# A hybrid decoder layer on one core: first key tiles finished in turn, short products between input steps, log-decay rows spread by DMA

## The chip, the cores and the metric

The kernel runs on one core of a Trainium2 chip. The metric is the time on the device in microseconds, the median of several runs; lower is better. The engines are TensorE (PE in the profile, PEld for its weight loads), VectorE (DVE), ScalarE (ACT), GpSimd (POOL) and SyncE (SP), whose queue issues all DMAs. Each engine takes its own instructions in the order in which they stand in the program, and waits at an instruction until the semaphores it names have been raised.

## What is computed

One layer of a decoder trunk for 1024 tokens of width 1024, all in float32. The part that matters here is the input projection and the preparation of the gated delta rule (4 heads of width 128):

```python
h = rmsnorm(x, norm1_w)
proj = h @ w_in                       # q, k, v, z (512 each), b, a (4 each), then 3 x 512 for mixer B
qkv_a = silu(causal_dwconv(qkv_a, conv_qkv_w))            # four taps
qa, ka = l2norm(q) * 128 ** -0.5, l2norm(k)
beta = sigmoid(b_a)
g = -exp(a_log) * softplus(a_a + dt_bias)                 # log decay per token and head
o_a = gated_delta_rule(qa, ka, va, g, beta)
...
gc = cumsum(g) within a chunk
dec = exp(gc[t] - gc[j]) for t >= j, else 0
lmat = strict(dec) * (k k^T) * beta                       # then a triangular solve, a scan over chunks
```

Behind it come dilated attention over the same projection, the output projection with a residual, a second norm, a gated MLP with a short convolution, a residual and a final norm.

## The kernel before

**Products.** Activations lie transposed, features on the partitions. A float32 product is made of three passes: operands are split into a rounded high part and a rest (`split`, lines 189 to 191; `split_x`), and `mm3` (lines 183 to 187) multiplies high x high, high x low and low x high into one bank of PSUM. In the profile such a pass is a `128x512` MATMUL of about 0.4 us that starts every 0.23 us, here called a wide product. Products that are not split (`mm`, `tp`) run as two passes for a float32 product and one for a transpose.

**The order of the work.** The program is recorded by generators which a small planner, `Weave` (lines 41 to 113), steps in turn. Each generator yields how long it wants to wait; the planner keeps an estimate of TensorE's time (`pe`) and of when each tile is ready, and runs the ready generator of the lowest level. `until(name)` waits for a named event, `need(tile)` gives the estimated wait for a tile, `slack` adds to it. What is recorded on TensorE stands in that order in the program (`TOKEN` is stamped on every product). The other engines' orders are made by a scheduler, so they aren't always those of the source.

**The first stage.** `first` (lines 313 to 321) multiplies the first three key column tiles: for each of the 8 feature tiles `k` it goes through the 3 tiles and 2 halves of the tokens (`pst`, six banks), so all six banks end with the last `k`. That is 144 wide products. Between them come, at levels 0 and 1:

- `norms` (lines 327 to 344): sums the squares over the features with products by a column of ones (`ssp`, 8 products of one column), takes the reciprocal root on POOL (`rst`), transposes it to rows over all partitions (8 transposes) and copies it to `rstdB`.
- `gates` (lines 351 to 388): the projection of the 8 gate columns (`wba`), evicted to `barow`, turned by 8 products with `sel`, then `beta` and `g` on DVE and ACT, and a product with the triangle `tri` that gives the running sums `gc`, with tokens on the partitions.

**Keys.** When `first` and `norms` are done, `dense` (line 438) adds `first_keys` (lines 431 to 436): the three pairs of banks are scaled by `rstdB` into `xr`, then each is put through `conv_silu` (lines 402 to 415): one ACT copy with a scale (the first tap), three DVE taps, a tanh on ACT, and a DVE step that makes `kT`. `dense` itself goes on with the other columns of the projection (`DENSE`, lines 37 and 38: key 3, two columns of mixer B, then q and v of head 0 and so on), 48 wide products each, in the two banks `hf`; the first of them are also the first two banks of `pst`.

`kprep` (lines 496 to 551), one for each head, waits for `gates` and makes the decay matrix `dec`: the head's `gc` is spread over all partitions by 8 TensorE transposes into two `atr` banks; ACT adds the negated `gc` as a bias, chunk by chunk; `gel`, the last column, is copied by DVE; POOL masks; ACT takes the exponential. Then `tokens` (lines 477 to 494) transposes `kT` through two more `atr` banks; ACT evicts each bank to `ktok` and takes four squares with sums from it (`sq`, into `ssk`). Then `kT` is multiplied with itself (two banks, four products each) and DVE makes `um` with `bp` and `dec`; four DMAs write its blocks to `mdram`. When all four heads are done, `forward_sub` solves the blocks on DVE. The tag `atr` has two banks in all: a new bank waits for the last reader of the bank before the last.

Of the kernel before, what the change touches and what calls it, by code (L numbers as in the profile page):

```python
# [7 lines left out]
F32 = mybir.dt.float32  # L8
F32R = mybir.dt.float32r
AF = mybir.ActivationFunctionType  # L10
# [5 lines left out]
P = 128  # L16
S = 1024
KT = 8
H = 4
NCH = 8  # L20
FT = 22
NEG = -1.0e30
EPS = 1e-6
SLOTS = {"kT": 2, "kU": 2, "dv": 2, "dw": 2, "kt": 4, "uy": 5, "qa": 4, "ev": 2, "go": 2, "Xa": 7, "Xb": 9}
TURNS = {"kT*": ("kT", "kU"), "dv*": ("dv", "dw"), "X": ("Xa",) * 7 + ("Xb",) * 9}
# [109 lines left out]
def hybrid_layer(tc, I, out):  # L135
# [14 lines left out]
    def tile_(pool, shape, dt, name, tag, bufs):  # L150
        return wv.slot(pool.tile(list(shape), dt, name=name, tag=tag, bufs=bufs), tag, bufs)
# [23 lines left out]
    def mm(dst, lhs, rhs, us, start=True, stop=True, **kw):  # L175
        tc.stamp_issue_order_token(nc.tensor.matmul(dst, lhs, rhs, start=start, stop=stop, **kw).ins, TOKEN)  # L176
        wv.product(us, dst, lhs, rhs)

    def tp(dst, src):
        tc.stamp_issue_order_token(nc.tensor.transpose(dst, src, ident).ins, TOKEN)  # L180
        wv.product(0.11, dst, src)

    def mm3(dst, lhs, rhs, first, last, **kw):
        us = 0.2135 * rhs[0].shape[-1] / 512
        mm(dst, lhs[0], rhs[0], us, first, False, **kw)
        mm(dst, lhs[0], rhs[1], us, False, False, **kw)
        mm(dst, lhs[1], rhs[0], us, False, last, **kw)
# [25 lines left out]

    mixer = dp.tile([8, P, S], F32, name="mixer")
    mdram = dp.tile([H, 32, 1024], F32, name="mdram")
    xdram = dp.tile([H, 32, 1024], F32, name="xdram")
    xtdram = dp.tile([H, 32, 1024], F32, name="xtdram")
    apark = dp.tile([4, 3, P, S], F32, name="apark")
# [8 lines left out]
    def next_bank(tag, *tiles, slack=0.0):  # L227

        while max(wv.need(*tiles), wv.slot_free(tag, 2)) + slack > 1e-3:
            yield max(wv.need(*tiles), wv.slot_free(tag, 2)) + slack  # L230
        return bank(tag)

    def half(i):
        return slice(i * 512, i * 512 + 512)

    def v8(t):
        return t.rearrange("p (c t) -> p c t", c=NCH)
# [73 lines left out]
    pst = [bank(t) for t in ("hf", "asc", "ch") for _ in range(2)]  # L311

    def first():
        for k in range(KT):
            w = wk0[k // 2]
            for i in range(6) if k else (0, 2, 4, 1, 3, 5):
                yield wv.need(*xs[k], *w)
                m, h = divmod(i, 2)
                wm = [t[:, k % 2, m * P:(m + 1) * P] for t in w]
                mm3(pst[i], wm, [t[:, half(h)] for t in xs[k]], k == 0, k == KT - 1)  # L320
        wv.done.add("first")


# [3 lines left out]
    def norms():  # L327
        yield wv.need(acc, slack=10.0)
        ssp = yield from next_bank("atr", acc)
        for c in range(NCH):  # L330
            mm(ssp[:, c:c + 1], acc[:, c * P:(c + 1) * P], ones[:, :1], 0.215)
            if c % 2:
                yield 0.4
        ve.tensor_scalar(rst, ssp[:, :NCH], 1.0 / 1024, EPS, op0=OP.mult, op1=OP.add)
        rsqrt(rst, rst, NCH)
        wv.done.add("rst")
        yield wv.need(rst)
        for h in range(2):
            pb = yield from next_bank("atr")
            for c in range(4):  # L340
                i = 4 * h + c
                tp(pb[:, c * P:(c + 1) * P], rst[:, i:i + 1].to_broadcast([P, P]))
            ve.tensor_copy(rstdB[:, half(h)], pb)
        wv.done.add("norms")
# [6 lines left out]
    def gates():  # L351

        yield wv.need(wba, xts[-1], slack=4.0)
        for h in range(2):
            pt = yield from next_bank("atr", wba, xts[-1])
            for k in range(KT):
                o = 32 * (k % 4)
                mm(pt[o:o + 32], wba[:, k, :], xts[k][:, half(h)], 0.3, k < 4, k >= 4, tile_position=(0, o))
            ac.activation(barow[:, half(h)], pt, AF.Copy)
        pt = yield from next_bank("atr", barow)  # L360
        for c in range(NCH):
            mm(pt[:, c * 8:(c + 1) * 8], barow[:, c * P:(c + 1) * P], sel, 0.215)
        yield from wv.until("rst")
        ba = sp.tile([P, NCH, 8], F32, name="ba")
        ve.tensor_tensor(ba, pt[:, :64].rearrange("p (c j) -> p c j", c=NCH),
                                rst[:, :, None].to_broadcast([P, NCH, 8]), op=OP.mult)
        ac.activation(beta, ba[:, :, :H], AF.Exp, scale=-1.0)
        ve.tensor_scalar(beta, beta, 1.0, None, op0=OP.add)
        ve.reciprocal(beta, beta)
        zt = sp.tile([P, NCH, H], F32, name="zt")  # L370
        ve.tensor_tensor(zt, ba[:, :, H:], dtb[:, None, :].to_broadcast([P, NCH, H]), op=OP.add)
        az = sp.tile([P, NCH, H], F32, name="az")
        ac.activation(az, zt, AF.Abs)
        ac.activation(az, az, AF.Exp, scale=-1.0)
        ac.activation(az, az, AF.Ln, bias=1.0)
        ve.scalar_tensor_tensor(az, zt, 0.0, az, op0=OP.max, op1=OP.add)
        ea = sp.tile([P, H], F32, name="ea")
        ac.activation(ea, alog, AF.Exp)
        g = sp.tile([P, NCH, H], F32, name="g")
        ve.scalar_tensor_tensor(g, az, -1.0, ea[:, None, :].to_broadcast([P, NCH, H]), op0=OP.mult,  # L380
                                       op1=OP.mult)
        pt = yield from next_bank("atr", g)
        mm(pt[:, :NCH * H], tri, g.rearrange("p c h -> p (c h)"), 0.215)
        ve.tensor_copy(gc, pt[:, :NCH * H].rearrange("p (c h) -> p c h", c=NCH))
        ve.tensor_scalar(ngc, gc, -1.0, None, op0=OP.mult)
        ac.activation(ngam, gc, AF.Exp)
        ve.tensor_scalar(ngam, ngam, -1.0, None, op0=OP.mult)
        wv.done.add("gates")
# [39 lines left out]
    T = {}  # L428
    gated = {}

    def first_keys():
        xr = [scaled(pst[2 * h:2 * h + 2], "xr", tag=("ev", "ev", "qa")[h]) for h in range(3)]
        for h in range(3):
            T["k", h] = conv_silu(xr[h], 4 + h, "kT", "kT*")
            wv.add(3, kprep(h))
            yield wv.need(T["k", h])

    def dense():

        yield from wv.until("first")  # L440
        yield from wv.until("norms")
        wv.add(2, first_keys())
        nxt = None
        for i, col in enumerate(DENSE):
            kind, h = col[:2]
            if kind == "z":
                yield from wv.until(("o", h))
            w = nxt or wk(I["wi"][i])
            if i + 1 < len(DENSE):
                nxt = wk(I["wi"][i + 1])  # L450
            pair = []
            for hh in range(2):
                pt = bank("hf")
                yield wv.need(pt, *w)
                for k in range(KT):
                    mm3(pt, [t[:, k, :] for t in w], [t[:, half(hh)] for t in xs[k]], k == 0, k == KT - 1)
                    yield 0.0
                pair.append(pt)
            if kind == "k":
                T["k", h] = conv_silu(pair, 4 + h, "kT", "kT*")  # L460
                wv.add(3, kprep(h))
            elif kind == "q":
                q = conv_silu(pair, h, "qT", "qa")
                wv.add(4, qprep(h, q))
            elif kind == "v":
                v = conv_silu(pair, 8 + h, "vT", "qa")
                wv.add(4, vprep(h, v))
            elif kind == "z":
                og = gated[h] = A("og", "kT*")
                sy.dma_start(og, mixer[h])  # L470
                ve.tensor_tensor(og, og, silu2(pair, "zz"), op=OP.mult)
            else:
                sy.dma_start(apark[h, col[2]], scaled(pair, "aqkv", True))
                wv.done.add(col)
        wv.done.add("dense")
# [20 lines left out]
    def kprep(h):  # L496
# [5 lines left out]
        dec = A("dec", ("dv", "dw")[h % 2])  # L502
        gend = small("gend")
        gel = small("gel")
        for hh in range(2):
            c0 = 4 * hh
            pg = yield from next_bank("atr")
            for c in range(4):
                tp(pg[:, c * P:(c + 1) * P], gc[:, c0 + c, h:h + 1].to_broadcast([P, P]))
            pv = pg.rearrange("p (c t) -> p c t", c=4)  # L510
            for c in range(4):
                ac.activation(v8(dec)[:, c0 + c, :], pv[:, c, :], AF.Identity, bias=ngc[:, c0 + c, h:h + 1])
            ve.tensor_copy(gel[:, c0:c0 + 4], pv[:, :, P - 1])
        po_.affine_select(v8(dec), v8(dec), pattern=[[0, NCH], [1, P]], compare_op=OP.is_ge, fill=NEG,
                                base=0, channel_multiplier=-1)
        ve.tensor_tensor(gend, gel, gc[:, :, h], op=OP.subtract)
# [958 lines left out]
```

## Time and profile before

| | |
|---|---|
| median of three runs | 1268.12 us (1267.27 to 1270.15) |
| the profiled execution: time, span | 1267.09 us, 1263.9 us |
| its mean granted TensorE clock | 0.992 |

A run of a profile lists busy time by engine, the span in 40 slices, the chain of work that ended last, and groups of instructions. Line 131 is the helper that records every DVE, ACT, POOL and SP operation, line 176 the one for products and line 180 the one for transposes, so instructions are told apart by their tiles: `kT<-xr,gcw,kT` is a tap of the convolution, `sq<-ps` a square with its sum, `dec<-ps,ngc` the decay with its bias, `xr<-ps,rstdB` the scaling.

The stage that the change touches lies in the first 120 us. Busy time of each engine there, in us, and TensorE's granted clock, from the view of windows:

| window, us | PE | DVE | ACT | clock |
|---|---|---|---|---|
| 20 to 30 | 9.84 | 9.30 | 5.61 | 1.00 |
| 30 to 40 | 9.05 | 2.20 | 2.01 | 0.74 |
| 40 to 50 | 10.00 | 2.93 | 3.06 | 0.92 |
| 50 to 60 | 10.00 | 10.00 | 6.71 | 1.00 |
| 60 to 70 | 8.03 | 10.00 | 8.38 | 0.95 |
| 70 to 80 | 10.00 | 8.68 | 4.52 | 0.88 |
| 80 to 90 | 10.00 | 5.69 | 4.87 | 1.00 |

All the waits of TensorE in the whole span sum to some 16 us; the largest are 2.8 us for `w` of the chunk chains, 2.1 for the second norm, 2.0 in the last product and 2.0 for `xr`, which is at 66 us.

### The profile page before, as it was taken

To read this page: it belongs to the slowest core of one execution; us is meant where nothing else is said; L and a number is where in the kernel's file an instruction comes from. 1 tells how busy PE (TensorE), PEld (TensorE's weight loads), DVE (VectorE), ACT (ScalarE), POOL (GpSimd) and SP (SyncE) were. 2 spreads that over 40 slices of the span, in tenths; PEclk is the share of its full clock that TensorE was granted. 3 is DMA by queue.
4 is the path that set the end of the run, shared out by engine and by line. 5 is a ranking of instruction groups with operands and counts; after the bars stand their busy time and mean duration, and the time that the engine had idled before them with its cause. 6 is when DMAs were issued, how large, how long until landed. Compare 5 with 4: busy or idle time off the path is not lost.

```text
span 1263.9 us, 18352 instructions
## 1 busy us (share of the span) xinstructions
PE 1240.5 (98%) x7102; PEld 1010.7 (80%) x7102; DVE 940.6 (74%) x1450; ACT 587.5 (46%) x1122; POOL 45.3 (4%) x34
## 2 busy tenths in 40 slices
PE   9999999999999999999999999999999999999996
PEld 7878887888677767878888888888888888787886
DVE  7575984573554455576888988988988979899875
ACT  7355534363544253365554444445445444343541
POOL 0012010022000000000000000000000000000000
PEclk9899999999999999999999999999999999999998
DMA  7022243345322411444323123123122198455623
GB/s 232 28 59 76 101 121 98 134 151 201 103 81 93 141 53 41 126 150 150 117 67 100 60 90 100 56 95 101 53 98 100 50 339 311 149 158 191 199 85 134
DMA packets 77766, 151.41 MB, mean 120 GB/s; under 512 B 21744, under 2 KB 28528, under 8 KB 77680
## 3 DMA queue, kind: packets, MB, share of 16 engines
q1 hardware_dynamic: 77680, 150.25, 36.1%
q8 instruction: 55, 0.90, 0.3%
q14 instruction: 31, 0.25, 0.1%
HBM read 112.21 MB, written 35.91 MB: 117 GB/s over the span
## 4 chain that ended last, share of the span: by engine, by line
PE 81%; DVE 8%; DMA 5%; issue 3%; ACT 2%; SPq 0%; POOL 0%; POOLq 0%; DVEq 0%; ACTq 0%
PE ps L176 42%; PE pa L176 18%; PE pc L176 9%; PE dw L176 8%; PE ps L180 4%; DMA wd<-in_wd 2%; DVE pr L131 2%; DMA r<-upark 1%; DVE x1h L131 1%; DVE kT L131 1%; DVE wd L131 1%; DVE r L131 0%; DMA wst<-in_wu 0%; DVE xr L131 0%; DMA xt<-in_xT 0%
## 5 line engine op out<-in xcount | busy, mean ns | idle before, releaser
L176 PE MATMUL dw<-pr 128*128 128x512 f32 (+1 forms) x984 | 213.4, 377 | 2.8 <-DVE x1h L131 2.0
L176 PEld LDWEIGHTS dw<-pr 128*128 128x128 f32 x984 | 176.1, 188 | 39.1 <-DVE x1h L131 4.2
L176 PE MATMUL ps<-xhi,whi 128*128 128x512 f32 x448 | 187.5, 419 | 2.0 <-DVE xr L131 2.0
L176 PE MATMUL ps<-xhi,wlo 128*128 128x512 f32 x448 | 177.0, 395 | 0.2 <-DVE wlo L131 0.2
L176 PE MATMUL ps<-xlo,whi 128*128 128x512 f32 x448 | 176.4, 394 | 0.0
L176 PE MATMUL pa<-T,pair 128*128 128x512 f32 x528 | 128.6, 393 | 0.7 <-ACT u L131 0.7
L176 PEld LDWEIGHTS pa<-T,pair 128*128 128x128 f32 x528 | 99.8, 189 | 21.8 <-ACT u L131 1.0
L176 PEld LDWEIGHTS ps<-xhi,whi 128*128 128x128 f32 x448 | 85.5, 191 | 19.4 <-issue 3.1
L176 PEld LDWEIGHTS ps<-xhi,wlo 128*128 128x128 f32 x448 | 85.0, 190 | 19.4 <-DVE wlo L131 0.6
L176 PEld LDWEIGHTS ps<-xlo,whi 128*128 128x128 f32 x448 | 85.7, 191 | 13.9
L131 ACT ACTIVATE u<-pa 128x512 f32<-128x512 f32 x44 | 26.3, 599 | 110.6 <-PE pa L176 110.6
L131 DVE SCALAR_TENSOR_TENSOR y<-xu,fcw,y 128x1023 f32<-128x1023 f32 (+1 forms) x44 | 56.4, 1281 | 25.7 <-ACT y L131 25.6
L131 ACT ACTIVATE whi<-wst 128x1024 fp32r<-128x1024 f32 (+2 forms) x38 | 38.6, 1016 | 68.8 <-PE ps L176 58.3
L176 PE MATMUL pa<-B,A 128*128 128x512 f32 x264 | 63.4, 389 | 0.0
L176 PE MATMUL pc<-T,S 128*128 128x512 f32 x264 | 63.4, 389 | 0.0
L176 PE MATMUL pa<-T,S 128*128 128x512 f32 x264 | 63.4, 389 | 0.0
L176 PE MATMUL pc<-B,pair 128*128 128x512 f32 x264 | 63.4, 389 | 0.0
L131 ACT ACTIVATE sm<-sm,mx 128x512 f32<-128x512 f32 (+2 forms) x64 | 41.5, 649 | 42.4 <-DVE mx L131 42.4
L131 DVE TENSOR_TENSOR wst<-wst 128x512 f32<-128x512 f32 x88 | 60.4, 686 | 0.8
L176 PE MATMUL ps<-B,pair 128*128 128x512 f32 x252 | 60.5, 389 | 0.0
L176 PEld LDWEIGHTS pc<-B,pair 128*128 128x128 f32 x264 | 49.6, 188 | 10.3
L176 PEld LDWEIGHTS pa<-B,A 128*128 128x128 f32 x264 | 49.6, 188 | 10.3
(233 smaller groups left out, 2280.4 us busy)
## 6 DMA issues: line engine op xcount, KB each, us to landing
wst<-in_wu SPq DMA_DIRECT2D x44, 512.0 KB, 3.6
wd<-in_wd SPq DMA_DIRECT2D x44, 512.0 KB, 4.0
wst<-in_wi SPq DMA_DIRECT2D x25, 512.0 KB, 3.7
upark<-y SPq DMA_DIRECT2D x22, 512.0 KB, 3.5
apark<-aqkv SPq DMA_DIRECT2D x12, 512.0 KB, 2.9
r<-upark SPq DMA_DIRECT2D x11, 512.0 KB, 7.9
r<-upark SPq DMA_DIRECT2D x22, 256.0 KB, 7.0
wa<-in_wd SPq DMA_DIRECT2D x22, 256.0 KB, 2.7
```

The costliest lines, as they stand in the source:

```text
L131: return getattr(eng, op)(*a, **kw)
L176: tc.stamp_issue_order_token(nc.tensor.matmul(dst, lhs, rhs, start=start, stop=stop, **kw).ins, TOKEN)
L180: tc.stamp_issue_order_token(nc.tensor.transpose(dst, src, ident).ins, TOKEN)
```

## The change

1. `first` takes its 144 wide products in another order: for the first five feature tiles (`TOGETHER`) as before, then key tile by key tile through the last three. The banks of tile 0 end 36 products before those of tile 2. As soon as a tile's second bank has ended, `first_key` for this head is added to the planner; it waits for `norms`, scales, convolves, and adds `kprep`. `first_keys` and its place in `dense` are gone.
2. In `norms` the 8 products with `ones` yield 0.6 us after each one (before: 0.4 us after each second one); in `gates` the 8 products with `sel` do too (before: none between them), and wait 2 us more for `barow`.
3. `gates` makes `gc` a second time with tokens along the row, by a product with the operands exchanged (32 rows: chunk and head). ACT evicts it to `grow`, and a DMA writes it to `gdram` in memory (16 KB). `kprep` no longer transposes: one DMA for each head reads the head's 8 rows of 512 bytes for all 128 partitions (a step of 0 over the partitions) into `dec`, 512 KB. `gel` is copied from there, and ACT adds the bias in place.

Computed values stay the same.

```diff
+TOGETHER = 5
...
+    gdram = dp.tile([NCH * H, P], F32, name="gdram")
...
     def first():
-        for k in range(KT):
+        steps = [(k, i) for k in range(TOGETHER) for i in (range(6) if k else (0, 2, 4, 1, 3, 5))]
+        steps += [(k, 2 * m + h) for m in range(3) for k in range(TOGETHER, KT) for h in range(2)]
+        for k, i in steps:
             w = wk0[k // 2]
-            for i in range(6) if k else (0, 2, 4, 1, 3, 5):
-                yield wv.need(*xs[k], *w)
-                m, h = divmod(i, 2)
-                wm = [t[:, k % 2, m * P:(m + 1) * P] for t in w]
-                mm3(pst[i], wm, [t[:, half(h)] for t in xs[k]], k == 0, k == KT - 1)
+            yield wv.need(*xs[k], *w)
+            m, h = divmod(i, 2)
+            wm = [t[:, k % 2, m * P:(m + 1) * P] for t in w]
+            mm3(pst[i], wm, [t[:, half(h)] for t in xs[k]], k == 0, k == KT - 1)
+            if k == KT - 1 and h == 1:
+                wv.add(2, first_key(m))
         wv.done.add("first")
...
             mm(ssp[:, c:c + 1], acc[:, c * P:(c + 1) * P], ones[:, :1], 0.215)
-            if c % 2:
-                yield 0.4
+            yield 0.6
...
+        yield wv.need(barow, slack=2.0)
         pt = yield from next_bank("atr", barow)
         for c in range(NCH):
             mm(pt[:, c * 8:(c + 1) * 8], barow[:, c * P:(c + 1) * P], sel, 0.215)
+            yield 0.6
...
-        mm(pt[:, :NCH * H], tri, g.rearrange("p c h -> p (c h)"), 0.215)
+        g32 = g.rearrange("p c h -> p (c h)")
+        mm(pt[:, :NCH * H], tri, g32, 0.215)
+        mm(pt[:NCH * H, P:2 * P], g32, tri, 0.215)
+        grow = tile_(sp, [NCH * H, P], F32, "grow", "osq", 1)
+        ac.activation(grow, pt[:NCH * H, P:2 * P], AF.Copy)
+        sy.dma_start(gdram, grow)
...
-    def first_keys():
-        xr = [scaled(pst[2 * h:2 * h + 2], "xr", tag=("ev", "ev", "qa")[h]) for h in range(3)]
-        for h in range(3):
-            T["k", h] = conv_silu(xr[h], 4 + h, "kT", "kT*")
-            wv.add(3, kprep(h))
-            yield wv.need(T["k", h])
+    def first_key(h):
+        yield from wv.until("norms")
+        xr = scaled(pst[2 * h:2 * h + 2], "xr", tag=("ev", "ev", "qa")[h])
+        T["k", h] = conv_silu(xr, 4 + h, "kT", "kT*")
+        wv.add(3, kprep(h))
 
     def dense():
         yield from wv.until("first")
         yield from wv.until("norms")
-        wv.add(2, first_keys())
...
-        for hh in range(2):
-            c0 = 4 * hh
-            pg = yield from next_bank("atr")
-            for c in range(4):
-                tp(pg[:, c * P:(c + 1) * P], gc[:, c0 + c, h:h + 1].to_broadcast([P, P]))
-            pv = pg.rearrange("p (c t) -> p c t", c=4)
-            for c in range(4):
-                ac.activation(v8(dec)[:, c0 + c, :], pv[:, c, :], AF.Identity, bias=ngc[:, c0 + c, h:h + 1])
-            ve.tensor_copy(gel[:, c0:c0 + 4], pv[:, :, P - 1])
+        rows = gdram.rearrange("(c h) t -> h c t", h=H)[h]
+        sy.dma_start(v8(dec), bass.AP(tensor=rows.tensor, offset=rows.offset, ap=[[0, P]] + list(rows.ap)))
+        ve.tensor_copy(gel, v8(dec)[:, :, P - 1])
+        for c in range(NCH):
+            ac.activation(v8(dec)[:, c, :], v8(dec)[:, c, :], AF.Identity, bias=ngc[:, c, h:h + 1])
```

## The prediction

> **What bounds the kernel now.** I read the page first: its engine table, its slices, its chain of waits. Columns of the first rows: busy us, share of the span, instructions.
>
> ```profile
> span 1263.9 us, 18352 instructions
> PE 1240.5 (98%) x7102; PEld 1010.7 (80%) x7102; DVE 940.6 (74%) x1450; ACT 587.5 (46%) x1122; POOL 45.3 (4%) x34
> PEclk9899999999999999999999999999999999999998
> PE 81%; DVE 8%; DMA 5%; issue 3%; ACT 2%; SPq 0%; POOL 0%; POOLq 0%; DVEq 0%; ACTq 0%
> ```
>
> TensorE sets the time: a microsecond put into its stream or taken out of it shows at the end, and what other engines do costs nothing unless TensorE waits for it. The clock is below full in slices 1 and 2, where the change lies, so I took TensorE's timeline there (start, duration, engine, form; in brackets the idle time before and who ended it):
>
> ```profile
> 31.41 1.95 PE L176 MATMUL ps<-sel,barow 128*128 128x8 f32 x16 [0.95 <-ACT barow L131]
> 35.40 0.63 PE L176 MATMUL ps<-xlo,whi 128*128 128x512 f32 x1
> 35.82 0.63 PE L176 MATMUL ps<-xhi,wlo 128*128 128x512 f32 x1
> 42.63 1.03 PE L180 MATMUL ps<-ident,rst 128*128 128x128 f32 x8
> 52.65 1.03 PE L180 MATMUL ps<-ident,gc 128*128 128x128 f32 x8
> 53.44 0.47 PE L176 MATMUL ps<-xhi,whi 128*128 128x512 f32 x1
> 65.33 0.66 PE L180 MATMUL ps<-ident,kT 128*128 128x128 f32 x4
> 67.95 0.50 PE L176 MATMUL ps<-xhi,whi 128*128 128x512 f32 x1 [1.97 <-DVE xr L131]
> 115.74 0.47 PE L176 MATMUL ps<-xhi,whi 128*128 128x512 f32 x1
> ```
>
> I count the wide products (128x512) of the input projection from the start. An undisturbed one takes 0.227 us (start to start). After 0.95 us of idling and 16 short `sel` instructions they take 0.427, from 34.8 to 41.4; after 1.97 us of idling again, from 68.8 to 72.1. Product 144, the last of the first three key tiles, ends at 52.65. Product 337 starts at 115.74: by then all four heads' keys are turned and multiplied in either version. That is my common mark.
>
> **What the change removes on TensorE.** (a) Sixteen one-column and eight-column products now stand one or two between steps of three wide ones. I take 0.2 us each (group of two `ones` at 33.22 to 33.67: 0.225; at 34.44 to 34.82: 0.19) and 0.09 for each return to wide products (33.67 to 33.98 is 0.31 instead of 0.227). From 29.96: two steps of 0.97, six of 1.17, two of 0.97 and one of 0.68 bring TensorE to the `rst` transposes at 41.5 (before 42.6); 0.87 for those, nine products, 0.43 for the two `tri` products (the new one by the nearest row, a 128-wide `kT` product at 0.2) and 18 products end product 144 at 49.1 (before 52.65): 3.5 gained, if the clock holds. (b) The `gc` transposes go: 2 x 0.88 and 4 x 0.45 = 3.6. (c) The 1.97 wait and its slow stretch (eleven products and four transposes, some 1.9) go: 3.9. Together 11.0.
>
> **What it adds: the order.** In the changed program's order, whose waits can be read off it, head 0's eight `kT` transposes stand on TensorE directly behind product 144, and product 145, the first of the next column, behind them. Before, 48 wide products and eight `gc` transposes stood there, 12.7 us of cover. TensorE takes them in order, and the first waits for DVE's last step on `kT`. When is that? DVE's timeline of before gives the prices:
>
> ```profile
> 43.27 1.29 DVE L131 COPY rstdB<-ps 128x512 f32<-128x512 f32 x2 [1.24 <-PE ps L180]
> 49.45 3.41 DVE L131 TENSOR_TENSOR xr<-ps,rstdB 128x512 f32<-128x512 f32 x5 [2.87 <-PE ps L176]
> 57.94 3.65 DVE L131 SCALAR_TENSOR_TENSOR kT<-xr,gcw,kT 128x1022 f32<-128x1022 f32 x3
> ```
>
> `rstdB` starts 0.64 after the transposes: 42.2. Behind it on DVE stand, in this order up to the third tap of head 0: two copies (1.3), six scalings (0.68 each, 4.1), five taps of heads 0 and 1 (1.2 each, 6.0), and `gc`, `ngc`, `ngam` (0.45): 42.2 + 11.8 = 54.0. ACT's tanh takes 1.06; meanwhile DVE does both `gel` copies, one tap each of heads 1 and 2, two `gend`: 57.0. The last step (1.2, and 0.8 more where POOL's mask runs beside it: a tap at 65.19 beside the mask at 64.92 takes 2.03) ends at 58.2 to 59.0. So **TensorE stands from 49.1 to about 58.7: 9.6 us**. Had the clock not held in (a), it would stand less by as much; only `rstdB`'s start matters.
>
> **Second stop.** Behind the transposes (0.9) come twelve wide products (2.7, or 5.1 at the slow clock), then `kT` times `kT`, which waits for the bank of the first four transposes. The order names its last reader: ACT's fourth `sq`. ACT's queue is the same for everything, and now the decays of all four heads stand ahead of it:
>
> ```profile
> 53.28 2.18 ACT L131 ACTIVATE dec<-ps,ngc 128x128 f32<-128x128 f32 x8
> 56.84 1.06 ACT L131 ACTIVATE dec<-dec 128x1024 f32<-128x1024 f32 x1 [0.33 <-POOL dec L131]
> 72.04 0.28 ACT L131 ACTIVATE sq<-ps 128x128 f32<-128x128 f32 x1
> 72.44 0.28 ACT L131 ACTIVATE sq<-ps 128x128 f32<-128x128 f32 x1
> 83.78 0.58 ACT L131 ACTIVATE ktok<-ps 128x512 f32<-128x512 f32 x1
> ```
>
> From the end of head 0's tanh at 55.1: 32 biased copies at 0.26 (8 in 2.18; they now read SBUF, bounds 0.19 to 0.28), 8.3; four exponentials at 1.0, 4.0; two tanh, 2.0; two `ktok`, 1.1; four `sq` with their read-outs, 0.40 from start to start, 1.6; six small ones, 0.9. Sum 17.9: **the bank is free at 73.0** (70.8 to 73.7). TensorE got there at 62.3 to 64.7, so it stands 8 to 11 us more. Heads 1 to 3 follow without such a stop, as ACT then has only their own `ktok` and `sq`; one wait is left at head 3: a weight split on ACT (1.05) waits for product 240 and holds back `ktok`, four `sq` and the second `ktok`, 3.9 us in all, while TensorE has 2.3 us of work: 1.6.
>
> **From 73.0 to the mark**: 180 wide products (156 to 336) x 0.227 = 40.8; eight groups of four `kT` products x 0.91 = 7.3; six groups of four transposes x 0.455 = 2.7; the wait 1.6; switches and small waits that before's own stretch from 75.59 shows over this count, 0.5. After a stop of eight microseconds I charge a slow stretch: before's two lasted 6.6 and 3.3 us at half rate, costing 3.1 and 1.6; I take 2.4. Mark at 73.0 + 52.9 + 2.4 = 128.3 against 115.7: **+12.6**, say +12. The gains of 11.0 are in it; the two stops of some 19, the 1.6 and the 2.4 outweigh them.
>
> For the 1.6 us wait, too, the clock must be asked. Idling of 1.97 us before the product at 67.95 was followed by the slow stretch; 1.16 at 275 was not (clock 1.00 there). So 1.6 may cost 0 to 1.9, and I leave it in the range. In the Trainium skill, TensorE: Matmul & The Clock Gate, Part 1, the clock falls after an idle window of about 3.4 us; by that rule the 1.6 would cost nothing, and the stretch after 1.97 should not have been slow. This trace does not agree with it.
>
> **The DMAs.** SP has issued its four weight loads by 32 (each slot's wait ends with a `wlo`, the second at 32.1), so the `gdram` row, evicted by ACT at 46.2, goes at once. 16 KB: 1.7 us as for a 32 KB `mdram` write. Each head's 512 KB comes in 512-byte runs, which no row shows; bounds are 3.6 (`wst`, 4 KB runs) and 7.9 (`r`, 512 KB under load). At 3.6 they land from 52 on, even one behind the other by 52, 55.6, 59.2 and 62.8; `gel` of head 0 asks at 54.0, of head 1 at 54.2, of heads 2 and 3 after 60 and 63. That is hidden by the DVE taps, but for 1.4 at most at head 1; I take 3.6 and nothing, since it is the same queue and size. At 7.9 one behind the other: 56, 64, 72, 80; then `gel` of head 1 holds DVE to 64, and ACT's decays of head 3 start at 80 instead of 67.7: +12. The write of `um` waits for DVE anyway and costs nothing.
>
> **Behind the mark** both orders have the same products; the chains' idle time (2.8 us waiting for `w`) may move by 2 either way. The forward substitution starts some 9 us ahead of the mark instead of 10 behind it, so the merges have more room, not less. From product 1008 on both stand alike: nothing gives the 12 us back, as TensorE is busy throughout.
>
> **Forecast.** The profiled execution took 1267.1 (span 1263.9 and 3.2 around it), 1.0 under the median 1268.1. 1267.1 + 12.6 = 1279.7: **1280 us**, chance 0.66.
>
> **Rivals.**
> *The broadcast loads are slow* (7.9 each, one behind the other). For: new 512-byte runs, all reading the same 4 KB per head. Against: 128-byte runs of 32 KB land in 1.7. Gives 1267 + 12 + up to 12: 1284 to 1291. Chance 0.16.
> *The clock falls in the spread narrow stretch as well.* For: it fell after the block of short instructions; against: a wide product now lies between every two. Transposes 1.4 later, and so all behind: 1281. Chance 0.08, inside the range.
> *Faster: the cover holds.* If TensorE's next wide products run while head 0's `kT` is made, the 11.0 of gains stand alone: 1257. It needs the transposes' operand by 49.1, nine microseconds before DVE's sum allows, and the bank by 61; it decides the sign once both stops together stay under 9. For: ACT and DVE are idle for long stretches from 31 to 49. Against: the order itself. Chance 0.06. Stops half as long: no difference, 0.04.
>
> **Numbers.** Range 1273 to 1289: below by the cheaper copies (-2.2), a short slow stretch (-0.8), chains (-2) and shorter stops; above by one or two late loads (+5), more slow clock (+2) and chains (+2). A measurement of this kernel tells 0.2% (2.5 us) from nothing. Faster 0.06, same 0.04, slower 0.90.
>
> **What would show it.** Right: TensorE idle some 9 us before the `kT` transposes, released by DVE `kT`, and again 8 to 11 before the first `kT` product, released by ACT `sq`; no idle time at `barow`; full clock from 30 to 49; ACT busy without gaps from 54 to 73; product 337 near 128. Wrong: DVE's `gel` or ACT's `dec` released by DMA (loads late), or TensorE without idle time at 49.

## The result and the profile after

| | before | after |
|---|---|---|
| median of four runs on the same chip, us | 1268.02 (1267.27 to 1270.15) | 1283.39 (1280.62 to 1283.58) |
| profiled execution: time, span, us | 1267.09, 1263.9 | 1283.31, 1281.4 |
| its mean granted clock | 0.992 | 0.988 |

The changed kernel takes 1.0116 times as long, 95% interval 1.0099 to 1.0133: 15 us slower. 1280 was forecast, with a range of 1273 to 1289.

Line numbers of the helpers have moved by one: DVE, ACT, POOL and SP operations are now line 132, products 177, transposes 181. The page of the changed kernel:

```profile
span 1281.4 us, 18309 instructions
PE 1237.9 (97%) x7072; PEld 1009.1 (79%) x7072; DVE 939.0 (73%) x1446; ACT 589.7 (46%) x1123; POOL 46.0 (4%) x34
PEclk9889999999999999999999999999999999999998
PE 80%; DVE 7%; DMA 6%; issue 3%; ACT 3%; SPq 0%; POOL 0%; POOLq 0%; DVEq 0%; ACTq 0%
```

TensorE has 30 instructions fewer and is busy 2.6 us less than before, yet the span is 17.5 longer: the time is not work but waiting. The waiting stands in slices 1 and 2 (counted from 0), as TensorE's timeline there shows (start, duration, engine, form; in brackets the idle time before, and who ended it):

```profile
63.16 1.94 PE L181 MATMUL ps<-ident,kT 128*128 128x128 f32 x8 [12.18 <-DVE kT L132]
75.33 2.08 PE L177 MATMUL ps<-kT 128*128 128x128 f32 x8 [6.79 <-ACT sq L132]
79.77 1.20 PE L177 MATMUL ps<-kT 128*128 128x128 f32 x8
107.44 1.16 PE L177 MATMUL ps<-kT 128*128 128x128 f32 x8 [0.95 <-ACT sq L132]
129.78 0.39 PE L177 MATMUL ps<-xhi,whi 128*128 128x512 f32 x1
```

Two stops: 12.2 us before head 0's `kT` transposes, for DVE; 6.8 before the first `kT` product, for ACT's `sq`. The last line is wide product 337, the mark. Eight transposes take 1.94 after the first stop and eight products 2.08 after the second, instead of 1.05: the clock is low there. The view of windows says how low (start and end, length, busy time of PE, PEld, DVE, ACT and POOL with counts, granted clock, DMA share, GB/s):

```profile
40.00:50.00 10.00, 10.00 (x52) 8.25 (x52) 6.46 (x15) 4.91 (x9) 1.64 (x1) 1.00 0.02 4
50.00:60.00 10.00, 0.97 (x5) 0.47 (x3) 7.75 (x12) 6.22 (x15) 0.47 (x1) 0.81 0.74 192
60.00:70.00 10.00, 5.38 (x20) 4.38 (x20) 9.00 (x12) 9.75 (x27) 2.99 (x3) 0.68 0.11 19
70.00:80.00 10.00, 4.67 (x16) 4.09 (x17) 1.76 (x8) 6.96 (x27) 2.73 (x2) 0.66 0.00 0
```

From 40 to 50 us TensorE works without a gap at full clock (before: 0.74 from 30 to 40, 0.92 from 40 to 50); then come 30 us of which it works 11.

What did DVE and ACT do meanwhile? DVE's timeline:

```profile
55.90 0.16 DVE L132 COPY gel<-dec 128x8 f32<-128x8 f32 x1
58.31 0.17 DVE L132 COPY gel<-dec 128x8 f32<-128x8 f32 x1 [2.25 <-DMA dec<-gdram]
58.39 3.32 DVE L132 SCALAR_TENSOR_TENSOR kT<-xr,gcw,kT 128x1021 f32<-128x1021 f32 x2
61.80 1.21 DVE L132 SCALAR_TENSOR_TENSOR kT<-xr,kT 128x1024 f32<-128x1024 f32 x1
```

Head 0's last step on `kT` starts at 61.80. In front of it DVE stands 2.25 us for head 1's load, which head 0 has no use for. The two taps behind that wait take 3.32 us; POOL's mask stands beside them from 59.53 to 60.63. ACT's timeline:

```profile
57.03 2.43 ACT L132 ACTIVATE dec<-dec,ngc 128x128 f32<-128x128 f32 x8
65.19 1.28 ACT L132 ACTIVATE dec<-dec,ngc 128x128 f32<-128x128 f32 x4
70.63 2.14 ACT L132 ACTIVATE dec<-dec,ngc 128x128 f32<-128x128 f32 x7
72.77 1.05 ACT L132 ACTIVATE dec<-dec 128x1024 f32<-128x1024 f32 x1
73.96 1.05 ACT L132 ACTIVATE dec<-dec 128x1024 f32<-128x1024 f32 x1
74.93 0.26 ACT L132 ACTIVATE sq<-ps 128x128 f32<-128x128 f32 x1
```

The last of these is the fourth square, the last reader of the bank for which TensorE waits until 75.33. Biased copies and exponentials of all four heads stand ahead of it. Three groups of DMAs of the same kernel (count, size, median us from issue to landing):

```profile
wst<-in_wi SPq DMA_DIRECT2D x25, 512.0 KB, 3.6
xt<-in_xT SPq DMA_DIRECT2D x7, 512.0 KB, 9.1
dec<-gdram SPq DMA_DIRECT2D x4, 512.0 KB, 8.1
```

The 8.1 is not the price of one load by itself. All four `dec` loads are issued between 50.06 and 53.49 us and land at 55.7, 58.3, 60.0 and 62.0, so several are under way at once. The seven `xt` loads at the start, in runs of 4 KB, are issued as closely and take 9.1. The `wst` loads of this stretch are issued 2 to 4 us apart.

### The profile page after: what moved, and what is told of

It is laid out like the page before. It is cut to its first block, busy times and chain, and to the rows that moved or that the text cites. A ratio compares the mean times of both kernels' runs of the same rounds, so it can differ in the third digit from the quotient of the medians.

```text
span 1281.4 us, 18309 instructions
## 1 busy us (share of the span) xinstructions
PE 1237.9 (97%) x7072; PEld 1009.1 (79%) x7072; DVE 939.0 (73%) x1446; ACT 589.7 (46%) x1123; POOL 46.0 (4%) x34
## 4 chain that ended last, share of the span: by engine, by line
PE 80%; DVE 7%; DMA 6%; issue 3%; ACT 3%; SPq 0%; POOL 0%; POOLq 0%; DVEq 0%; ACTq 0%
PE ps L177 43%; PE pa L177 18%; PE pc L177 9%; PE dw L177 7%; PE ps L181 4%; DMA wd<-in_wd 2%; DVE pr L132 2%; DMA r<-upark 2%; DVE x1h L132 1%; DVE wd L132 1%; ACT sq L132 1%; DMA dec<-gdram 1%; ACT dec L132 1%; DVE kT L132 1%; DMA xt<-in_xT 1%
## 5 line engine op out<-in xcount | busy, mean ns | idle before, releaser
L132 DVE SCALAR_TENSOR_TENSOR y<-xu,fcw,y 128x1023 f32<-128x1023 f32 (+1 forms) x44 | 56.3, 1280 | 25.7 <-ACT y L132 25.6
L177 PE MATMUL ps<-B,pair 128*128 128x512 f32 x252 | 60.5, 389 | 0.0
L132 ACT ACTIVATE pr<-wd 128x1024 fp32r<-128x1024 f32 x33 | 35.0, 1059 | 52.8 <-DVE wd L132 33.6
```

The source lines that it names most:

```text
L132: return getattr(eng, op)(*a, **kw)
```

## The experiments

Waits set the time, and each can hide another, so I read every run at the mark and not only at its end. One thing had to be cleared up first: everything in the profile after starts 1.9 us later than in the profile before, already at product 79, which the change's later parts can't reach. The kernel before was therefore profiled again (last experiment): product 79 starts at 30.27 there too, and product 337 at 117.52. The marks below are counted from this second profile:

```profile
117.52 0.47 PE L176 MATMUL ps<-xhi,whi 128*128 128x512 f32 x1
```

Each ratio in the table is to runs of the kernel before on the same chip in the same session; its median there was 1268.0 to 1268.7. "First stop" is the idle time before head 0's `kT` transposes, "second stop" that before its first `kT` product.

| kernel | median, us | ratio to before, 95% interval | first stop | second stop | product 337 against before |
|---|---|---|---|---|---|
| after | 1283.39 | 1.0116 (1.0099 to 1.0133) | 12.18 | 6.79 | +12.3 |
| weights first | 1273.86 | 1.0042 (1.0022 to 1.0061) | 2.07 | 11.76 | +4.4 |
| decays held | 1275.97 | 1.0069 (1.0049 to 1.0090) | 11.50 | 2.99 | +7.6 |
| both | 1268.61 | 1.0004 (0.9987 to 1.0020) | 2.03 | 3.48 | -1.9 |
| both, more wait | 1262.90 | 0.9948 (0.9931 to 0.9966) | 0.55 | 1.94 | -5.4 |
| both, still more | 1267.50 | 0.9995 (0.9979 to 1.0011) | 0.92 | none | not comparable |
| `gel` later | 1280.22 | 1.0096 (1.0076 to 1.0116) | 8.83 | 9.78 | +12.2 |
| parts 1 and 2 | 1271.28 | 1.0033 (1.0016 to 1.0050) | 7.37 | none | +2.9 |
| parts 1 and 2, weights first | 1263.82 | 0.9967 (0.9954 to 0.9980) | none | 0.59 | -5.1 |
| part 1 alone | 1275.22 | 1.0057 (1.0033 to 1.0080) | none, but 3.85 at `gc` | none | +4.3 |
| part 2 alone | 1262.92 | 0.9959 (0.9944 to 0.9974) | none | none | -4.6 |
| part 3 alone | 1272.40 | 1.0036 (1.0023 to 1.0049) | 9.49 | 0.34 | +4.9 |

### Dense weights recorded first

The planner places head 0's transposes ahead of product 145 because, in its books, the split of the first dense weights stands behind the key convolutions on DVE and ACT. This edit records the split before them:

```diff
         for k, i in steps:
+            if (k, i) == (TOGETHER, 0):
+                wd.extend(wk(I["wi"][j]) for j in range(2))
             w = wk0[k // 2]
...
-            w = nxt or wk(I["wi"][i])
-            if i + 1 < len(DENSE):
-                nxt = wk(I["wi"][i + 1])
+            w = wd[i]
+            if 0 < i < len(DENSE) - 1:
+                wd.append(wk(I["wi"][i + 1]))
```

> The changed kernel, with the first two weight tiles of the dense columns split (recorded) before the key convolutions instead of behind them; nothing else differs. In the program TensorE now has 42 wide products more (up to number 186) between product 144 and head 0's kT transposes. ACT's order is otherwise as before: the decays of all four heads stand ahead of the fourth square. Theory (two causes: the transposes' place makes the first stop, ACT's queue of decays the second): product 186 ends at 50.8 + 42 x 0.227 = 60.3 in the changed kernel's times, kT is ready at 62.5, so the first stop shrinks from 12.2 to 2 or 3 us; the second grows, since the bank still comes free at 76 to 77 (75.3, and a weight split of 1.05 and a copy stand ahead of it now) while TensorE is there at 65: 10 to 12 us instead of 6.8. TensorE has 192 instead of 156 wide products behind it then: 36 x 0.227 - 1.7 = 6.5 gained, 1277 us (1274 to 1280). Rival (one cause: the order alone, the second stop follows from the first): both stops go, 1283.4 - 19 = 1264. Rival (the planner's order is no cause, kT is simply late): no gain, 1283.

TensorE's timeline of this run:

```profile
62.33 1.06 PE L181 MATMUL ps<-ident,kT 128*128 128x128 f32 x8 [2.07 <-DVE kT L132]
76.55 2.08 PE L177 MATMUL ps<-kT 128*128 128x128 f32 x8 [11.76 <-ACT sq L132]
```

The transposes start about when they did in the changed kernel (62.33 against 63.16), but 42 wide products have been done in the meantime. The second stop grows to 11.8, as ACT's queue is what it was. The time, 1273.9, is 3 us below the 1277 expected and just under its range: 1.3 of that at the mark, the rest behind it. Neither single-cause rival holds.

### Decays held

```diff
+        if h:
+            yield from wv.until(("t", h - 1))
...
         for c in range(NCH):
-            ac.activation(v8(dec)[:, c, :], v8(dec)[:, c, :], AF.Identity, bias=ngc[:, c, h:h + 1])
+            t = ac.activation(v8(dec)[:, c, :], v8(dec)[:, c, :], AF.Identity, bias=ngc[:, c, h:h + 1])
+            if h:
+                after(t, G[h - 1]["sq"])
```

`("t", h)` is done when head h's `tokens` are recorded; `G[h]["sq"]` is their last square.

> The changed kernel, but the biased copies of head 1's decay stand behind head 0's last square on ACT, those of head 2 behind head 1's and so on; loads, values and the place of head 0's kT transposes (behind product 144) are as in the changed kernel. TensorE's product kT with kT of head 0 comes directly behind the transposes here, without the 12 wide products between. Theory (ACT's queue of decays makes the second stop): the first stop stays at 12 us (11 to 13); then ACT has two ktok, four squares and one tanh to do, about 3.6 us, so the bank is free at 64.1 + 3.6 = 67.7 instead of 75.3: 144 products done at 67.7 instead of 156 at 75.3, that is 7.6 - 12 x 0.227 = 4.9 gained: 1278.5 (1276 to 1281). Rival (the bank of the transposes is late for another reason, such as DVE): no gain, 1283.

```profile
62.38 1.94 PE L181 MATMUL ps<-ident,kT 128*128 128x128 f32 x8 [11.50 <-DVE kT L132]
67.30 3.78 PE L177 MATMUL ps<-kT 128*128 128x128 f32 x16 [2.99 <-ACT sq L132]
```

In TensorE's timeline the first stop is nearly unchanged and the bank is free at 67.30 (67.7 expected) instead of 75.33. 4.7 us are gained at the mark (4.9 expected); the time, 1276.0, is at the lower end of its range. So it was ACT's order that set the end of the second stop.

### Both together

> Both of the two earlier edits together in the changed kernel: the dense columns' first two weight tiles recorded before the key convolutions, and the decays of heads 1 to 3 held on ACT behind the squares of the head before. Theory (two separate causes, so both gains come): first stop 2 us as with the first edit alone; then the transposes (0.9), six wide products (1.4), and ACT has two ktok, a weight split (1.05, which waits for product 192), a tanh, a copy and four squares to do: bank free at 69.0 instead of 76.55, second stop about 4 instead of 11.8. 1273.9 - 7.5 = 1266.4 (1264 to 1269), about the kernel before. Rival (both edits take away the same stop, so their gains don't add): 1274.

```profile
62.27 1.06 PE L181 MATMUL ps<-ident,kT 128*128 128x128 f32 x8 [2.03 <-DVE kT L132]
69.29 2.07 PE L177 MATMUL ps<-kT 128*128 128x128 f32 x8 [3.48 <-ACT sq L132]
```

69.29 where 69.0 was expected. At the mark the two edits gain 7.8 and 4.7 alone and 14.2 together: two causes, and a little more than the sum, since with the weights first alone 5 us of the gain went to the second stop. That takes back the loss: the change with its order mended is as fast as the kernel before.

### More waiting before the transposes

Both edits, and 6 us instead of 3 in `yield wv.need(kT, slack=SLACK)` of `kprep`; the second run also adds 2.5 us to the wait for each bank of the `kT` products.

> As the run with both edits (weight tiles first, decays held), and the planner waits 3 us more before each head's kT transposes: head 0's stand behind product 192, its kT times kT behind 204. Theory: first stop under 1 us, second 1 to 2, and no slow clock behind them, so the mark (product 337) comes at 111 to 112 where the run with both edits had 115.6; behind the mark 0 to 3 us go to waits of the chains: 1264.5 (1261 to 1267), beside 1262.9 of part 2 alone. Rival (the place of the transposes no longer matters, since DVE and ACT are the bound there): 1268.

> As the run with both edits, but the planner is told to wait 3 us more before each head's kT transposes and 2.5 us more before each bank of kT times kT. Head 0's transposes then stand behind product 192, and its kT times kT only behind 288, with the transposes of heads 1 to 3 before it. Theory: first stop under 1 us, no second; some 2 us of waiting at head 2's transposes, whose bank waits for head 1's squares behind one decay; the gains of 11 (spread, gc transposes, xr wait) then stand nearly whole: 1268 - 11 + 3 = 1260 (1257 to 1264). Rival (something else in the new parts costs several us, such as the loads' DMA traffic): 1264 or more although the waits are gone.

The first gives 1262.90. Its mark is 5.4 us ahead of before, of the 11 that the three parts were to gain; the remaining waits (0.55 and 1.94, 0.79 for `xr`) and one slow stretch are the most of the rest. Behind the mark it loses 3.6 of the 5.4 up to product 1009 and ends, in the median, level with part 2 alone. The second is a miss: the stops are gone, but its `kT` products now lie around the mark, and TensorE waits 5.8 us in five waits for squares on ACT (some at head 1 to 3's transposes, some later). 1267.5 is where its rival stood, though not for the rival's reason.

### `gel` behind head 0's `kT`

```diff
-        ve.tensor_copy(gel, v8(dec)[:, :, P - 1])
+        t = ve.tensor_copy(gel, v8(dec)[:, :, P - 1])
+        if h:
+            after(t, lastk[0])
```

`lastk[0]` is head 0's last step on `kT`.

> The changed kernel, but on DVE the copies of gel for heads 1 to 3, which wait for their loads, stand behind head 0's last step of kT instead of before it. TensorE's and ACT's orders and all loads are as in the changed kernel. Theory (the first stop holds 2.25 us of DVE waiting for head 1's load, but the second stop ends with ACT's queue, which doesn't care): kT is ready 2 us earlier, first stop 10 instead of 12.2, second stop 9 instead of 6.8, the fourth square still ends at 75 to 76, and the time is unchanged: 1283 (1281 to 1284). Rival (what is taken from the first stop is gained at the end): 1281 or less, with the second stop at 6.8. Rival (the wait for the load isn't on the chain to kT): first stop still 12.

```profile
59.93 1.94 PE L181 MATMUL ps<-ident,kT 128*128 128x128 f32 x8 [8.83 <-DVE kT L132]
75.10 2.07 PE L177 MATMUL ps<-kT 128*128 128x128 f32 x8 [9.78 <-ACT sq L132]
```

TensorE's timeline: 3.4 us less at the first stop, 3.0 more at the second, and product 337 at 129.74 instead of 129.78. What is taken from the first of two waits in a row goes to the second. `kT` is ready 3.2 us earlier and not 2: besides the 2.25, the two taps now lie ahead of POOL's mask, as DVE's timeline shows (3.32 us for them in the changed kernel):

```profile
56.09 2.47 DVE L132 SCALAR_TENSOR_TENSOR kT<-xr,gcw,kT 128x1021 f32<-128x1021 f32 x2
```

The median is 3.2 us lower all the same, just under the lowest run of the changed kernel (its runs: 1280.62 to 1283.58) and under the range that was expected. The intervals of the two ratios overlap, so whether the edit gains anything is not settled. Product 1105 starts at the same time in both profiles (439.76 and 439.77); the 3.5 us between the two profiled executions arise behind it, and 1.6 of them are a fall of the clock that one execution has and the other has not (last section).

### The parts by themselves

Parts 1 and 2 without part 3, and the same with the weights first:

> The changed kernel without its third part: the decays are spread by TensorE transposes of gc again, no row is written to memory and none is loaded; the first tiles still end one behind the other and the short products are spread. Head 0's kT transposes stand behind product 150, eight gc transposes before them. Theory: kT is ready some 2.3 us earlier (the wait of gel for its load is gone) and TensorE comes 1.8 + 1.4 later, so the first stop is 4 to 7 us instead of 12.2; there is no second stop, as ACT has only head 0's decay ahead of its squares; the gc transposes cost 3.6 again. 1268 - 3.5 (spread) - 3.9 (wait for xr) + 5.5 + 1.6 (slow clock) = 1267.7 (1264 to 1271). Rival (the third part is harmless, the order alone costs): first stop of 9 or more and a second of 6 stay, 1283 + 3.6 = 1286.

> Parts 1 and 2 without part 3 (decays by TensorE transposes), and the dense columns' first two weight tiles recorded before the key convolutions: kT transposes of head 0 behind product 192, gc transposes behind 150. Theory: TensorE is at the kT transposes at 50.1 + 48 x 0.227 + 1.8 = 62.5 to 63 and kT was ready at 59.9 in the run of parts 1 and 2, so no first stop; ACT has one head's decay ahead, so no second; the xr wait of before is gone too, since the scalings run from the first tile's end: 1262.9 (part 2 alone) - 2 to - 3.6 = 1260 (1258 to 1263). Rival (part 1 in itself costs, by DVE being loaded earlier): 1266 or more.

Without the loads `kT` is ready at 59.90 instead of 63.16, and the second stop is gone. But the first stop is 7.4 (4 to 7 expected), and 1271.3 is 3.6 above the sum; the longer stop and a wait of 1.26 at later `gc` transposes, which the sum did not have, are the most of it. With the weights first nearly no stop is left (0.59). 1263.8 misses the 1260 expected: part 1 neither costs nor gains much over part 2 alone (1262.9), and its mark is only 0.5 ahead.

> The kernel before with part 2 alone: the 16 short products of norms and gates lie one or two between input steps. Theory: the idle time before the sel products and the slow clock behind them go, product 144 ends 3.5 us earlier, and DVE's scalings, which wait for it, too, so the rest of the stage shifts as a whole: 1264.5 (1263 to 1266). Rival (what is gained there is lost again at the next wait, since kT hangs on rstdB and DVE and not on product 144): 1268.

> The kernel before with part 1 alone: key tiles end one behind the other, short products bunched and decays by TensorE transposes as before. Head 0's kT transposes stand behind product 150, behind the gc transposes of two heads. Theory (part 1 takes TensorE's cover away and brings kT only little earlier, so the stop is kT's time less TensorE's): in the times of the second profile of before, product 144 ends at 54.4, two times eight gc transposes and six products bring TensorE to the kT transposes at 57.6; kT was ready at 59.9 in the run of parts 1 and 2 and rstdB comes 1.3 later here: 61.2. First stop 3.6 us instead of 7.4, no second stop. 1268.2 - 3.9 (wait for xr and its slow stretch) + 3.6 + 1.6 (slow clock) = 1269.5 (1267 to 1272), 8 us less than part 1 cost on top of part 2. Rival (part 1 costs the same with and without part 2): 1268.2 + 8.4 = 1276.6.

> The kernel before with part 3 alone: decays by DMA, no gc transposes; tiles end together, short products bunched. Head 0's kT transposes stand behind product 189, 45 wide products of cover. Theory (part 3 lets ACT take the decays of all four heads before the squares, whatever the order of the tiles): TensorE is at the transposes at 62.9 in the times of before; kT of head 0 stands behind all nine taps on DVE and is ready at about 68, first stop 5; its squares stand behind the four decays, bank free at about 77, second stop 5 or 6. 1268 - 3.6 (gc transposes) - 3.9 (wait for xr) + 10.5 + 3 (slow clock) = 1274 (1270 to 1277). Rival (part 3 hurts only together with the early keys, else it is the saving of the transposes): 1264.5.

Part 2 alone, in TensorE's timeline:

```profile
49.81 1.04 PE L180 MATMUL ps<-ident,gc 128*128 128x128 f32 x8
65.11 0.50 PE L176 MATMUL ps<-xhi,whi 128*128 128x512 f32 x1 [1.97 <-DVE xr L131]
```

In the second profile of before:

```profile
54.42 1.03 PE L180 MATMUL ps<-ident,gc 128*128 128x128 f32 x8
69.73 0.50 PE L176 MATMUL ps<-xhi,whi 128*128 128x512 f32 x1 [1.97 <-DVE xr L131]
```

The whole stage moves forward by 4.6, with its 1.97 us wait unchanged. The gain is kept to the end; the kernel runs at 0.9959 of before.

Part 1 alone was a miss. Its TensorE timeline:

```profile
57.30 0.65 PE L181 MATMUL ps<-ident,gc 128*128 128x128 f32 x4 [0.60 <-DVE gel L132]
61.20 0.95 PE L181 MATMUL ps<-ident,gc 128*128 128x128 f32 x4 [3.25 <-DVE gel L132]
64.51 1.19 PE L181 MATMUL ps<-ident,kT 128*128 128x128 f32 x8
```

The stop is 3.9 us long, near the 3.6 expected, but at the `gc` transposes, whose banks wait for `gel` copies behind taps on DVE; `kT` is ready by the time they are over. The mark is 4.3 later, 3 more than the sum's 1.3. Two of these 3 are there when product 144 ends, at 56.7 where the theory took 54.4: the granted clock is 0.70 and 0.78 from 30 to 40 and 40 to 50 us, 0.82 and 0.84 in the second profile of before. On top of part 2, part 1 costs 7.5 at the mark (2.9 + 4.6), so it costs less alone, as the theory says, but by 3 us and not by 8. The median, 1275.2, lies 6 us above 1269.5 and near the rival's 1276.6, which it does not exclude: 5.6 us more are lost between the mark and product 1009, with waits of 1.19 for `x` in a merge and 1.66 for `pb`, and a clock of 0.74 from 210 to 230 us.

Part 3 alone stops once, in TensorE's timeline:

```profile
74.92 1.94 PE L180 MATMUL ps<-ident,kT 128*128 128x128 f32 x8 [9.49 <-DVE kT L131]
```

A stop of 9.5 and one of 0.3 stand where 5 and 5.5 were expected: DVE is later than I reckoned, so ACT is done by then. DVE's timeline shows why:

```profile
55.55 0.17 DVE L131 COPY gel<-dec 128x8 f32<-128x8 f32 x1 [2.31 <-DMA dec<-gdram]
57.85 0.17 DVE L131 COPY gel<-dec 128x8 f32<-128x8 f32 x1 [0.85 <-DMA dec<-gdram]
62.25 1.05 DVE L131 COPY gel<-dec 128x8 f32<-128x8 f32 x1
```

Two waits for loads, and a copy of eight columns that takes 1.05 us while POOL's mask runs (61.86 to 63.28). 1272.4 fits the 1274 expected, by another split than the sum's. So the saving of the `gc` transposes is lost even with the tiles in their old order.

### The kernel before, once more

> The kernel before, profiled a second time. In its first profiled execution product 79 starts at 28.45 us, in those of all the other kernels at 29.8 to 30.4, though nothing before it differs but the order of products. If that is chance, product 79 starts at about 30 here too and the span is some 1.5 us longer than 1263.9; if the other kernels cause it, at 28.4 again.

Product 79 at 30.27, span 1264.3, 1267.12 us. The early start of the first profile was chance, and it was given back later in the same execution.

## Why the prediction was right

Times of the prediction are those of the first profile of before; 1.8 us are added where they are compared with a start in a later profile.

- **Short products spread (+3.5), clock held.** Right. Product 144 starts 3.6 us earlier than in the second profile of before; the clock is 1.00 from 20 to 50 us. Part 2 alone gives 4.6, of which 0.45 is there at product 79 already. The rival that the clock falls there is out.
- **First stop, 9.6.** Right in place and cause, 2.6 too small. The term that failed is that of the DMAs: "At 3.6 they land from 52 on ... I take 3.6 and nothing". Head 1's load landed at 58.3; loads of 3.6 one behind the other would have given 55.6 + 1.8 = 57.4, the 1.4 that the text allowed and then put at nothing. `gel` of head 1 held DVE for 2.25, and the taps behind it took 0.85 more beside POOL's mask. With that copy moved away `kT` was ready at 59.9; the sum of taps alone had said 58.7 + 1.8 = 60.5. So one of the text's own signs of being wrong appeared, `gel` released by a DMA. It cost some 3 us at the first stop and then nothing, as the second stop absorbs it. The rival with 0.16 did not come as it was told, with loads of 7.9 one behind the other and the last at 80: the loads overlapped and the last landed at 62.0.
- **Second stop, 8 to 11, bank free at 73.0.** The bank was free at 75.3, with the shift of 1.8 half a microsecond later than forecast; the copies from SBUF came every 0.29 us and not every 0.26. The stop was 6.8 only because the first was longer. The sum of both, 19.0, is the "some 19" of the text.
- **Wait of 1.6 at head 3.** 0.95, with the clock at 1.00 behind it.
- **The mark, +12.6.** +12.3 against the second profile of before; product 337 was to start near 128, with the shift near 129.8, and starts at 129.78. The late bank (0.5) and the shorter wait at head 3 (0.65) nearly cancel. The slow stretch behind the second stop, charged with 2.4, cost about that: the clock is 0.50 from the end of the stop to 80 us, 4.7 us of work.
- **"Behind the mark ... nothing gives the 12 us back."** This is what was missing from the forecast: 3.2 us more are lost between the mark and product 1009 (265.5 us, 262.2 before). With the 12.3 and the 1.6 of the last section they make up the 17.1 us between the two spans. The forecast also started from the profiled execution, 1 us under the median of before; that and the 3.2 are the most of what lies between 1280 and 1283.4. TensorE's timeline there:

```profile
195.73 1.76 PE L177 MATMUL ps<-qT,kT 128*128 128x128 f32 x8 [1.88 <-ACT sq L132]
369.72 1.09 PE L181 MATMUL ps<-ident,vT 128*128 128x128 f32 x8 [1.68 <-ACT pb L132]
```

  Together 3.6 us of waiting, and half clock from 196 to some 199 us, against 2.4 us of waits for the chains in before. The prediction had set 2 either way for this; of the kernels run, those with part 3 and that with part 1 alone lose 0.5 to 5.6 us there (leaving out the one whose `kT` products lie around the mark), the three others between -0.2 and 0.1. That they meet other gaps is shown; which order leads to which was not followed up.
- **The rule weighed.** In the Trainium skill, TensorE: Matmul & The Clock Gate, Part 1, the clock falls after an idle window of about 3.4 us. The runs disagree with a reading by the length of the idle time: half clock followed 1.97 us (part 2 alone), 1.94 (both, more wait) and 1.88 (changed kernel), but not 1.04 or 1.86 (both, still more). The same part of the Trainium skill says that the window is free-running; the section below has a row that fits this.
- **"The cover holds" (1257).** Its condition was missed in the changed kernel, and the run with weights first and old decays shows it met: no stop before the transposes, 0.59 behind them, 1263.8. That run keeps the `gc` transposes, so of the 11.0 it could have 7.4 (without their 3.6); its mark is 5.1 ahead.

## What to carry to other kernels

An order made by a planner hangs on its books: when work is recorded earlier, ask what now stands behind it in the planner's account, because a product may lose its place for a wait that exists only there. Making an operand earlier on a busy engine and taking work off TensorE gained nothing here, as the first product that needed the operand lost its cover and the engine that evicts the banks got other work ahead of the eviction. Read two waits in a row as one: time taken from the first shows at the second until both causes are mended.

## What the runs showed of the hardware

- The granted clock fell in one execution and not in another of the same stretch. TensorE's products are in the same order in the changed kernel and in the run with `gel` later; windows of 2 us, first the changed kernel:

```profile
492.00:494.00 2.00, 1.82 (x30) 1.25 (x16) 2.00 (x5) 0.65 (x3) 0.00 (x0) 0.77 0.36 147
494.00:496.00 2.00, 2.00 (x16) 1.67 (x14) 1.24 (x5) 1.28 (x3) 0.00 (x0) 0.50 0.03 8
```

  and the run with `gel` later, whose clock stays at 1.00:

```profile
492.00:494.00 2.00, 1.82 (x37) 1.25 (x23) 2.00 (x5) 0.64 (x3) 0.00 (x0) 1.00 0.37 150
494.00:496.00 2.00, 2.00 (x20) 1.38 (x16) 1.95 (x7) 1.28 (x3) 0.00 (x0) 1.00 0.03 8
```

  It costs 1.6 us there; runs of one kernel differ by 3 us or more.
- Half clock sets in late: after the 1.97 us wait that ends at 65.11 with part 2 alone, the clock is 1.00 until 66, then 0.62 and 0.53 in the next two windows of 2 us.
- Four loads of 512 KB in runs of 512 bytes, the same eight for every partition, issued within 3.4 us, took 5.6 to 8.8 us to land, 1.7 to 2.6 apart. The `xt` loads of the same size in runs of 4 KB, issued one after the other at the start, landed mostly 1.3 apart. Loads in runs of 4 KB that are issued further apart took 3.6. How much of the difference the short runs make, and how much the source that is read 128 times, is not shown.
- A DVE instruction beside POOL's mask can take about 1 us more: `gel` 1.05 instead of 0.16 (part 3 alone), a tap 2.0 instead of 1.27 (before).
